# RWKV-7 stage of a one-core hybrid block: token shift, key scaling and decays read PSUM or go through ScalarE

## The chip, the core and the metric

One core of one Trainium2 chip runs one transformer block in fp32: sequence 1024, model width 1024. The metric is the device time of the whole program in microseconds, the median of the runs taken. TensorE multiplies, VectorE and ScalarE and GpSimd work on rows of 128 partitions, and DMA queues move data between HBM and the on-chip memory SBUF. TensorE writes its results to PSUM, a memory of eight banks of 128 x 512 fp32, from which VectorE and ScalarE read them.

In the profile the engines are PE (TensorE matmul), PEld (its weight loads), DVE (VectorE), ACT (ScalarE), POOL (GpSimd) and SP. L424 is line 424 of the kernel, `rkv<-rraw` an output and its inputs by the program's names.

## The reference

The block is an RMS norm, one wide input projection, three mixers side by side (NSA attention, RWKV-7, a gated delta network called GDN), gates that merge them, an output projection and a feed-forward part. The change touches the RWKV-7 mixer alone:

```python
c = c + (_shift(c) - c) * mu                       # token shift of r, k, v, wd, ad, gd
r, k, v, wd, ad, gd = jnp.split(c, splits, axis=-1)
w = -jax.nn.softplus(-(w0 + jnp.tanh(wd) @ w_up)) - 0.5
decay = jnp.exp(-jnp.exp(w))
a = jax.nn.sigmoid(a0 + ad @ a_up)
g = jax.nn.sigmoid(gd) @ g_up
kk = _l2n(heads(k * k_k))
k = k * (1.0 + (a - 1.0) * k_a)
# scan over the tokens, a 64 x 64 state per head, 8 heads:
sa = jnp.einsum('bhij,bhj->bhi', state, -kk_t)
state = state * w_t + sa (kk_t * a_t) + v_t k_t
y_t = jnp.einsum('bhij,bhj->bhi', state, r_t)
# then a norm of y per head, the bonus sum(r * k * r_k) * v, and times g
```

`_shift` moves a sequence by one token and puts zero first, so the shift is `c[t] + (c[t-1] - c[t]) * mu`, the same as `c[t] * (1 - mu) + c[t-1] * mu`.

## The kernel before

Every dense fp32 product is made of three fp32r matmuls, from operands split into a high and a low part. The weights come by DMA (`wraw`), ScalarE casts the high part (`whi`, L254) and GpSimd, here and there VectorE, subtracts for the low part (`wlo`, L259). A projection tile is 128 columns by half the sequence, 512 tokens: two loads of weights with 12 matmuls each (4 slices of the depth times 3) into one PSUM bank called `fps`. Two banks serve for `fps`, two for the general tiles `mps` with the tag "m", and one each for four others.

The RWKV stage lies at about 50 to 600 us of the span. `mixed` (L419) makes one of its 28 projection tiles, 14 column tiles by two halves: two for the low-rank inputs `wa` and `gd`, then r, k and v for two groups of head pairs (`pp` 0 and 1). When a half is complete, `take` copies it from PSUM to `rraw` (L424, ScalarE), puts the last column of the half before in front (L425), keeps its own last column (L427), and VectorE forms the difference of neighbours (L428) and multiplies and adds (L429) to give `rkv`, `wa` or `gd`. There is one `rraw` buffer.

`_rwkv_unit` treats 256 tokens of one group; there are eight units, `u = 4 * pp + q`. A unit

- makes the decays: two small products with sigmoids (L506) give `sg` and `av`, a scan within chunks of 64 (`tensor_tensor_scan`, L511) gives `cs`, GpSimd subtracts `sg` from `cs` for the sum up to the token before (L513), and ScalarE's exponentials give `sg`, `AG`, `WI` and `wc` (L520 to L524);
- once its r and k are there, makes `kk` (L531), its square `sq` (L533), the first rows of `AG` (L537, L538), the scaled key `k2`, which the profile calls `k` (L541, L542), `rk` and `kk * av` on GpSimd (L544, L545), and the chunk-relative keys `BK` from `k2` and `kk` times `WI` (L550);
- on TensorE sums `sq` and `rk` over the heads and multiplies `AG` by `BK` (results taken at L585 to L587), inverts a triangular matrix per chunk by blocks, and runs the recurrence over the chunks (`VS` at L682, L699, L705), then the norm of the output.

Nobody writes the order by hand. The units are generators (`Task`). A planner, `run` with `dense_step`, resumes the unit that is due, using a clock of estimated TensorE time and the waits in the table `LAT`, and puts steps of the dense projections between them, in the share that `BESIDE` gives. Then a scheduler, which simulates the engines' time, sets the order of each engine's instructions. All engines work through their instructions in that order and wait at each for its inputs and for its output's buffer. Besides RWKV's own projections, the dense work between the units is that of GDN and the other branches.

Buffers that the change touches: `SABUF = 5` for the rotating 128 x 512 tiles `sg`, `cs`, `WI`, `kk`, `sq`, `k2`, `rk`; the single `rraw`; and the "m" banks.

Of the kernel before, what the change touches and what calls it, by code (L numbers as in the profile page):

```python
# [19 lines left out]
P = 128  # L20
# [13 lines left out]
KAPPA = math.exp(-0.5)  # L34
# [77 lines left out]
class Block:  # L112
# [82 lines left out]
    def constants(self):  # L195
        nc, c, a = self.nc, self.const, self.a
# [23 lines left out]
        for n, k in (("nsa_q_norm", 1), ("nsa_k_norm", 3)):  # L220
# [159 lines left out]
    def rwkv(self):  # L380
        nc, tc, a, wk = self.nc, self.tc, self.a, self.wk
        col = self.col

        gmask = self.tl("gmask", 1, [P, 2, 64])
        m16 = self.tl("m16", 1, [P, 64])
        for i in range(2):
            t, base = gmask[:, i], -i
# [5 lines left out]
        for t, blk in ((m16, 16),):  # L393
            nc.gpsimd.memset(t, 0.0)
            for h in range(2):
# [3 lines left out]
                for b in range(1, 64 // blk, 2):  # L399
# [4 lines left out]
                                            base=b * blk - 1, channel_multiplier=-1)  # L404
        cmask = self.tl("cmask", 1, [P, P])
# [47 lines left out]
        consts = (gmask, m16, cmask, sums)  # L453
        shared = {}
# [16 lines left out]
    def _rwkv_unit(self, u, jobs, rkv, wa, gd, consts, shared):  # L471
# [36 lines left out]
        sg, av = sgav
        cs = ta("cs")
        for x in (slice(i * P, i * P + P) for i in range(4)):  # L510
            nc.vector.tensor_tensor_scan(out=cs[:, x], data0=cmask, data1=sg[:, x], initial=0.0, op0=OP.mult, op1=OP.add)  # L511
        csc = ch(cs)
# [12 lines left out]

# [1089 lines left out]
```

## Time and profile before

| | |
|---|---|
| runs (3) | 2533.8, 2536.28, 2540.54 us; median 2536.28 |
| profiled execution | 2527.64 us, of which the span is 2525.9 |
| PE | 2377.5 us busy, 94% of the span |
| PEld | 1907.6 us, 76% |
| DVE | 1472.0 us, 58% |
| ACT | 1043.1 us, 41% |
| POOL | 986.8 us, 39% |
| mean granted TensorE clock | 0.965 |

The chain that ended last, followed back from the last instruction, lies to 72% on PE and to 13% on DVE. The span holds one profiled execution. A view by windows gives each engine's busy time in a stretch and the share of full speed that TensorE's clock was granted there; a view of waits gives how long an engine stood still and for whose result; a view by groups gives the mean duration of one kind of instruction.

### The profile page before, as it was taken

The page shows a single profiled execution, that of the slowest core. Times are in us where ns is not written, and L with a number is a line of the kernel's source. Part 1 is how long each engine was busy: PE and PEld are TensorE (multiplying, and loading weights), DVE is VectorE, ACT ScalarE, POOL GpSimd, SP SyncE. Part 2 cuts the span into 40 slices and gives each one's busy share as a digit, 9 for nine tenths or more (in the row PEclk, how much of TensorE's full clock was granted, in tenths as well). Part 3 has the DMA queues.
Part 4 walks back from the last instruction along what each step waited for, and adds up shares of the span by engine and source line. Part 5 has one row for each costly group of instructions (what it writes and reads, how often), then busy time and mean ns, then how long its engine had stood idle before and what let it go on. Part 6 is the DMA issues. An engine that isn't in the chain of part 4 may idle for free.

```text
span 2525.9 us, 37184 instructions
## 1 busy us (share of the span) xinstructions
PE 2377.5 (94%) x13589; PEld 1907.6 (76%) x13589; DVE 1472.0 (58%) x3197; ACT 1043.1 (41%) x2083; POOL 986.8 (39%) x975
## 2 busy tenths in 40 slices
PE   6979899999988999989999999999999998999999
PEld 4757676777776777777887777778888876788887
DVE  4586877663477567232556777766454436545444
ACT  5333433332344433225657665654332334423232
POOL 4444444333322121224545675344333346233232
PEclk9889889999999999989999999999999999999999
DMA  4222222222223122272213331014232354223232
GB/s 137 68 56 65 58 63 58 71 54 74 72 66 83 43 57 73 83 173 80 64 52 114 111 106 57 21 62 128 92 109 84 117 164 157 75 88 111 83 111 92
DMA packets 319718, 216.79 MB, mean 86 GB/s; under 512 B 78486, under 2 KB 273184, under 8 KB 319536
## 3 DMA queue, kind: packets, MB, share of 16 engines
q1 hardware_dynamic: 308672, 195.63, 27.3%
q10 hardware_dynamic: 9792, 17.83, 2.0%
q8 instruction: 107, 1.75, 0.3%
q0 software_dynamic: 1072, 0.96, 0.2%
q14 instruction: 75, 0.61, 0.1%
HBM read 178.16 MB, written 36.22 MB: 85 GB/s over the span
## 4 chain that ended last, share of the span: by engine, by line
PE 72%; DVE 13%; DMA 6%; ACT 4%; issue 2%; POOL 2%; SPq 0%; ACTq 0%; POOLq 0%; DVEq 0%
PE fps L97 53%; PE mps L97 15%; PE mps L101 3%; DVE inv_p L336 2%; DVE inv_u L338 1%; DVE gacc L882 1%; DVE BK L550 1%; DMA cw<-in_nsa_cmp_w_dram 1%; POOL wlo L259 1%; DMA lb<-inv 1%; ACT P L1349 1%; ACT whi L254 1%; DMA wraw<-in_w_branch_dram 1%; DVE ast L1344 1%; DMA gin<-gates 1%
## 5 line engine op out<-in xcount | busy, mean ns | idle before, releaser
L259 POOL TENSOR_TENSOR wlo<-wraw,whi 128x512 fp32r<-128x512 f32 (+2 forms) x408 | 530.0, 1302 | 878.9 <-ACT whi L254 848.5
L254 ACT CAST whi<-wraw 128x512 fp32r<-128x512 f32 (+1 forms) x408 | 286.6, 705 | 632.1 <-PE fps L97 444.8
L97 PE MATMUL fps<-hTh,whi 128*128 128x512 f32 x1024 | 447.3, 439 | 6.5 <-ACT rraw L424 3.5
L97 PE MATMUL fps<-hTh,wlo 128*128 128x512 f32 x1024 | 415.8, 410 | 1.3 <-POOL wlo L259 1.3
L97 PE MATMUL fps<-hTl,whi 128*128 128x512 f32 x1024 | 416.5, 408 | 0.0
L259 DVE TENSOR_TENSOR wlo<-wraw,whi 128x256 fp32r<-128x256 f32 (+1 forms) x207 | 129.7, 629 | 232.5 <-ACT whi L254 227.0
L97 PEld LDWEIGHTS fps<-hTh,whi 128*128 128x128 f32 x1024 | 200.9, 197 | 48.5 <-ACT rraw L424 3.6
L97 PEld LDWEIGHTS fps<-hTh,wlo 128*128 128x128 f32 x1024 | 200.0, 196 | 47.7 <-POOL wlo L259 2.2
L97 PEld LDWEIGHTS fps<-hTl,whi 128*128 128x128 f32 x1024 | 201.8, 197 | 32.3
L97 PE MATMUL fps<-h2h,whi 128*128 128x512 f32 x512 | 200.0, 391 | 1.3 <-DVE h2l L291 1.3
L1363 POOL TENSOR_SCALAR P<-P,ast 128x64 f32<-128x64 f32 (+5 forms) x128 | 137.2, 1088 | 160.0 <-DVE ast L1356 97.1
L97 PE MATMUL fps<-h2l,whi 128*128 128x512 f32 x512 | 199.6, 390 | 0.0
L97 PE MATMUL fps<-h2h,wlo 128*128 128x512 f32 x512 | 199.4, 390 | 0.0
L97 PE MATMUL fps<-whi,fl 128*128 128x512 f32 x512 | 191.0, 389 | 0.0
L97 PE MATMUL fps<-whi,fh 128*128 128x512 f32 x512 | 189.9, 391 | 0.0
L97 PE MATMUL fps<-wlo,fh 128*128 128x512 f32 x512 | 189.0, 389 | 0.0
L1442 DVE TENSOR_TENSOR acc<-fps,acc 128x512 f32<-128x512 f32 x160 | 106.7, 686 | 101.4 <-PE fps L97 101.0
L1349 ACT ACTIVATE P<-mps,ast 128x128 f32<-128x128 f32 (+4 forms) x256 | 124.9, 494 | 75.3 <-DVE ast L1347 45.5
L1344 DVE TENSOR_REDUCE ast<-mps 128x1 f32<-128x128 f32 (+4 forms) x256 | 109.0, 441 | 56.3 <-PE mps L97 53.5
L1392 DVE TENSOR_TENSOR PL<-mps,PH 128x512 fp32r<-128x512 f32 (+2 forms) x168 | 103.3, 619 | 47.7 <-ACT PH L1391 47.0
L1391 ACT CAST PH<-mps 128x512 fp32r<-128x512 f32 (+2 forms) x168 | 88.1, 533 | 63.5 <-PE mps L101 58.1
L97 PEld LDWEIGHTS fps<-h2h,whi 128*128 128x128 f32 x512 | 96.2, 188 | 21.5 <-DVE h2l L291 1.8
(465 smaller groups left out, 4802.0 us busy)
## 6 DMA issues: line engine op xcount, KB each, us to landing
wraw<-in_w_in_dram SPq DMA_DIRECT2D x152, 256.0 KB, 2.9
wraw<-in_w_ff_dram SPq DMA_DIRECT2D x128, 256.0 KB, 2.8
wraw<-in_w_ff_dram SPq DMA_DIRECT2D x64, 512.0 KB, 3.4
gates<-fst ACTq DMA_DIRECT2D x48, 256.0 KB, 2.0
wraw<-in_w_branch_dram SPq DMA_DIRECT2D x48, 256.0 KB, 3.2
gin<-gates SPq DMA_DIRECT2D x48, 256.0 KB, 3.2
wraw<-in_w_out_dram SPq DMA_DIRECT2D x16, 512.0 KB, 3.5
nsa_in<-fst ACTq DMA_DIRECT2D x20, 256.0 KB, 2.1
```

The source lines that it names most:

```text
L97: return self.note(self.nc.tensor.matmul(out, lhsT=lhsT, rhs=rhs, **kw))
L101: return self.note(self.nc.tensor.transpose(out, x, ident))
L254: nc.scalar.copy(hi, raw)
L259: eng.tensor_tensor(out=lo[:, x], in0=raw[:, x], in1=hi[:, x].bitcast(F32), op=OP.subtract)
L336: nc.vector.tensor_tensor(out=v, in0=lt[:n, s, None, s + 1:].to_broadcast([n, w, w]), in1=u[:n, s + 1:, s + 1:].rearrange("p t c -> p c t" ...
L338: nc.vector.tensor_reduce(out=u[:n, s, s + 1:], in_=v, axis=AX, op=OP.add)
L1344: nc.vector.tensor_reduce(out=(mx if i == 0 else mx2)[:, b:b + 1], in_=ps[:, :n], axis=AX, op=OP.max, negate=True)
L1349: nc.scalar.activation(out=Pt[:, c:c + n], in_=tiles[i][:, :n], func=AF.Exp, bias=mx[:, b:b + 1], accum_out=(sm if i == 0 else sm2)[:, b:b ...
L1363: eng.tensor_scalar(out=Pt[:, c:c + n], in0=Pt[:, c:c + n], scalar1=r[:, b:b + 1], scalar2=None, op0=OP.mult)
L1391: nc.scalar.copy(PH[:n, x0:x1], ps[:n, x0:x1])
L1392: tt(out=PL[:n, x0:x1], in0=ps[:n, x0:x1], in1=PH[:n, x0:x1].bitcast(F32), op=OP.subtract)
L1442: tt(out=acc[:, st, c0:c0 + 512], in0=ps, in1=acc[:, st, c0:c0 + 512], op=OP.add)
```

## The change

Token shift: ScalarE now writes `ps * (1 - mu)` from PSUM straight to the output (L434 of the changed kernel), and one VectorE instruction adds `mu` times the same PSUM bank moved by one column (L439). The first column of the second half comes from the edge by one ScalarE instruction (L438). `rraw` and the subtraction are gone. The PSUM bank is thus read by VectorE as the last reader. `1 - mu` and `1 - k_a` are made once at the start.

Decays: the sigmoids and the scan write tiles with a zero column ahead of every chunk (`sgl`, `csl`, 65 columns per chunk, one buffer each), so the sum up to the token before is the same tile read one column to the left, and GpSimd's subtraction is dropped.

Key scaling: `kk` goes from VectorE to ScalarE (L542). `k2` is `av * k_a + (1 - k_a)` on ScalarE (L552), then one multiplication by `k` on VectorE (L555). `WI`'s exponential goes into a PSUM bank with the tag "m", later in the unit (L554), and the `BK` products read it there (L563). `SABUF` falls from 5 to 4.

```diff
-SABUF = 5
+SABUF = 4
...
+        less = c.tile([P, 18], F32, name="less")
+        self.col["less_mu"], self.col["less_k_a"] = less[:, 0:14], less[:, 14:18]
...
+            for n, o in (("rwkv_mu", "less_mu"), ("rwkv_k_a", "less_k_a")):
+                nc.vector.tensor_scalar(out=self.col[o], in0=self.col[n], scalar1=-1.0, scalar2=1.0, op0=OP.mult, op1=OP.add)
...
+        cmask = self.tl("cmask", 1, [P, 2, 65])
         nc.gpsimd.memset(cmask, 1.0)
-        nc.gpsimd.memset(cmask.rearrange("p (c t) -> p c t", t=64)[:, :, 0:1], 0.0)
+        nc.gpsimd.memset(cmask[:, :, 0:1], 0.0)
+        lead = [self.tl(n, 1, [P, 8, 65]) for n in ("sgl", "csl")]
+        nc.gpsimd.memset(lead[0][:, :, 0:1], 0.0)
...
             def take(ps, half):
-                raw, o = self.tl("rraw", 1, [P, 513]), out(half)
-                nc.scalar.copy(raw[:, 1:513], ps)
-                nc.scalar.copy(raw[:, 0:1], edge)
+                o = out(half)
+                nc.scalar.activation(out=o, in_=ps, func=AF.Copy, scale=less)
                 if half == 0:
-                    nc.scalar.copy(edge, raw[:, 512:513])
-                nc.vector.tensor_tensor(out=o, in0=raw[:, 0:512], in1=raw[:, 1:513], op=OP.subtract)
-                nc.vector.scalar_tensor_tensor(out=o, in0=o, scalar=col["rwkv_mu"][:, ct:ct + 1], in1=raw[:, 1:513],
+                    nc.scalar.copy(edge, ps[:, 511:512])
+                else:
+                    nc.scalar.activation(out=o[:, 0:1], in_=edge, func=AF.Identity, scale=mu, bias=o[:, 0:1])
+                nc.vector.scalar_tensor_tensor(out=o[:, 1:512], in0=ps[:, 0:511], scalar=mu, in1=o[:, 1:512],
                                                op0=OP.mult, op1=OP.add)
...
-            o = ta("sg")
+            o = ch(ta("av")) if y else sgl[:, :, 1:65]
...
+        for i in range(4):
+            x = slice(2 * i, 2 * i + 2)
+            nc.vector.tensor_tensor_scan(out=flat(csl[:, x]), data0=flat(cmask), data1=flat(sgl[:, x]), initial=0.0,
+                                         op0=OP.mult, op1=OP.add)
...
-        nc.gpsimd.tensor_sub(sg, cs, sg)
...
-        WI = ta("WI")
+        sg = ta("sg")
...
-        nc.scalar.activation(out=sg, in_=sg, func=AF.Exp, scale=-KAPPA)
+        nc.scalar.activation(out=ch(sg), in_=before, func=AF.Exp, scale=-KAPPA)
...
-        nc.scalar.activation(out=WI, in_=cs, func=AF.Exp, scale=KAPPA)
...
-            ts(out=pr(kk)[:, x], in0=k[:, x], scalar1=one("rwkv_k_k", x), scalar2=None, op0=OP.mult)
+            nc.scalar.activation(out=pr(kk)[:, x], in_=k[:, x], func=AF.Copy, scale=one("rwkv_k_k", x))
...
-            ts(out=pr(k2)[:, x], in0=pr(av)[:, x], scalar1=1.0, scalar2=one("rwkv_k_a", x), op0=OP.subtract, op1=OP.mult)
-        stt(out=pr(k2), in0=pr(k2), scalar=1.0, in1=k, op0=OP.add, op1=OP.mult)
+            nc.scalar.activation(out=pr(k2)[:, x], in_=pr(av)[:, x], func=AF.Identity, scale=one("rwkv_k_a", x), bias=one("less_k_a", x))
+        WI = ps_tile()
+        nc.scalar.activation(out=ch(WI), in_=cs, func=AF.Exp, scale=KAPPA)
+        tt(out=pr(k2), in0=pr(k2), in1=k, op=OP.mult)
```

How the instructions of VectorE stand in a row at the first unit's keys, before (`k_854` is this unit's k2, `rkv` the r, k and v tiles):

```order
L428 TENSOR_TENSOR rkv<-rraw 128x512
L429 SCALAR_TENSOR_TENSOR rkv<-rkv,pcol,rraw 128x512
L531 TENSOR_SCALAR kk<-rkv,pcol 128x256
L428 TENSOR_TENSOR rkv<-rraw 128x512
L429 SCALAR_TENSOR_TENSOR rkv<-rkv,pcol,rraw 128x512
L531 TENSOR_SCALAR kk<-rkv,pcol 128x256
L537 SCALAR_TENSOR_TENSOR AG<-sg,kk 64x4x64 x4
L541 TENSOR_SCALAR k_854<-sg,pcol 128x256 x2
L542 SCALAR_TENSOR_TENSOR k_854<-k_854,rkv 128x512
L550 TENSOR_TENSOR BK<-kk,WI 64x8x64 x2
L550 TENSOR_TENSOR BK<-k_854,WI 64x8x64 x2
```

and in the changed kernel, from the tile that completes k to the last `BK` (`k_833` is k2, the `mps` read by L563 is `WI`):

```order
L439 SCALAR_TENSOR_TENSOR rkv<-fps,pcol,rkv 128x511 x2
L549 TENSOR_TENSOR AG<-rkv,AG 128x4x64 x2
L439 SCALAR_TENSOR_TENSOR rkv<-fps,pcol,rkv 128x511 x2
L548 SCALAR_TENSOR_TENSOR AG<-sg,kk 64x4x64 x4
L555 TENSOR_TENSOR k_833<-k_833,rkv 128x512
L563 TENSOR_TENSOR BK<-k_833,mps 64x8x64 x2
L563 TENSOR_TENSOR BK<-kk,mps 64x8x64 x2
L439 SCALAR_TENSOR_TENSOR rkv<-fps,pcol,rkv 128x511 x2
```

L428, L531 and L541 are gone from the row, L555 and L563 stand where L542 and L550 stood, and `AG` comes before one of the shift's instructions instead of behind it.

ScalarE at the same place before, from the last of unit 0's tiles that it copies to the square `sq`:

```order
L424 COPY rraw<-fps 128x512
L427 COPY edge<-rraw 128x1
L254 CAST whi<-wraw 128x512
L425 COPY rraw<-edge 128x1
L533 ACTIVATE sq<-kk 128x512
L254 CAST whi<-wraw 128x512
L424 COPY rraw<-fps 128x512
```

and in the changed kernel:

```order
L434 ACTIVATE rkv<-fps,less 128x512
L436 COPY edge<-fps 128x1
L542 ACTIVATE kk<-rkv,pcol 128x256
L259 CAST whi<-wraw 128x512 x2
L434 ACTIVATE rkv<-fps,less 128x512
L436 COPY edge<-fps 128x1
L542 ACTIVATE kk<-rkv,pcol 128x256
L259 CAST whi<-wraw 128x512
L544 ACTIVATE sq<-kk 128x512
L552 ACTIVATE k_833<-av,less,pcol 128x256 x2
```

`kk` and `k2` have joined ScalarE's row, with the casts of the next projections' weights among them; a shift tile is one L434 and one L436 where it was L424, L427 and L425.

VectorE at the start of the stage, before (`g_*` are GDN's decays, `wa` the first shift tile):

```order
L825 SCALAR_TENSOR_TENSOR g_p<-g_p,g_z 128x32
L827 SCALAR_TENSOR_TENSOR g_x<-g_p,g_x 128x32
L829 SCALAR_TENSOR_TENSOR g_g<-g_x,hc 128x32
L428 TENSOR_TENSOR wa<-rraw 128x512
L429 SCALAR_TENSOR_TENSOR wa<-wa,pcol,rraw 128x512
L682 COPY VS<-Z_640 64x2x64 x2
L428 TENSOR_TENSOR wa<-rraw 128x512
L429 SCALAR_TENSOR_TENSOR wa<-wa,pcol,rraw 128x512
```

and in the changed kernel:

```order
L838 SCALAR_TENSOR_TENSOR g_p<-g_p,g_z 128x32
L840 SCALAR_TENSOR_TENSOR g_x<-g_p,g_x 128x32
L842 SCALAR_TENSOR_TENSOR g_g<-g_x,hc 128x32
L439 SCALAR_TENSOR_TENSOR wa<-fps,pcol,wa 128x511 x2
L695 COPY VS<-Z_635 64x2x64 x2
L521 SCALAR_TENSOR_TENSOR csl<-cmask,sgl 128x130 x2
```

The shift of `wa` keeps its place behind the `g_*` row; it is now the instruction that frees the `fps` bank.

## Rows read from the trace of the kernel before

**Rows 1.** Window: length, busy PE, PEld, DVE, ACT, POOL, clock, DMA share, GB/s

```profile
50.00:600.00 550.00, 509.10 (x3907) 383.58 (x3909) 395.61 (x947) 196.24 (x378) 228.29 (x241) 0.92 0.26 63
```

**Rows 2.** PE's waits, 50 to 600 us: total us, times, longest us

```profile
PE mps L97 <- DVE VS L699: 8.0, 6, 2.4
PE mps L97 <- DVE BK L550: 7.4, 3, 4.0
PE mps L97 <- POOL rk L544: 5.2, 2, 3.5
...
PE fps L97 <- ACT rraw L424: 3.5, 1, 3.5
PE mps L97 <- DVE VS L682: 2.3, 1, 2.3
```

**Rows 3.** Windows at the start, behind stalls, without one (columns as rows 1)

```profile
53.00:60.00 7.00, 6.88 (x23) 5.52 (x24) 5.55 (x21) 1.53 (x6) 3.96 (x14) 0.76 0.15 34
60.00:70.00 10.00, 10.00 (x47) 7.30 (x46) 3.89 (x7) 8.07 (x17) 2.85 (x3) 1.00 0.11 27
108.00:122.00 14.00, 14.00 (x43) 10.32 (x43) 7.03 (x19) 1.53 (x5) 3.60 (x3) 0.51 0.15 37
145.00:153.00 8.00, 6.56 (x26) 5.50 (x26) 7.75 (x20) 0.19 (x1) 2.53 (x2) 0.57 0.25 66
278.00:293.00 15.00, 12.15 (x78) 10.24 (x79) 11.48 (x24) 3.58 (x7) 6.50 (x8) 0.54 0.25 56
408.00:419.00 11.00, 10.68 (x75) 9.17 (x76) 7.12 (x20) 3.27 (x5) 1.39 (x1) 0.53 0.14 35
508.00:562.00 54.00, 51.41 (x468) 38.11 (x467) 37.13 (x100) 19.74 (x34) 20.15 (x23) 1.00 0.27 63
```

**Rows 4.** DVE groups, 50 to 600 us: busy us, mean ns, idle before, releaser

```profile
L428 DVE TENSOR_TENSOR rkv<-rraw 128x512 f32<-128x512 f32 x24 | 25.2, 1051 | 20.5 <-ACT rraw L424 20.2
...
L429 DVE SCALAR_TENSOR_TENSOR rkv<-rkv,pcol,rraw 128x512 f32<-128x512 f32 x24 | 22.5, 939 | 0.6
L550 DVE TENSOR_TENSOR BK<-k,WI 64x512 f32<-64x512 f32 x16 | 20.0, 1248 | 0.4
L550 DVE TENSOR_TENSOR BK<-kk,WI 64x512 f32<-64x512 f32 x16 | 18.4, 1152 | 0.3
...
L541 DVE TENSOR_SCALAR k<-sg,pcol 128x256 f32<-128x256 f32 x16 | 14.8, 967 | 0.0
...
L531 DVE TENSOR_SCALAR kk<-rkv,pcol 128x256 f32<-128x256 f32 x16 | 8.1, 532 | 0.1
...
L542 DVE SCALAR_TENSOR_TENSOR k<-k,rkv 128x512 f32<-128x512 f32 x8 | 6.5, 809 | 0.2
```

**Rows 5.** Single lines: min/median/max ns, first and last start us, shape

```profile
L726 DVE TENSOR_TENSOR Y<-Y,gst x8: 676/693/1815, 226.0 to 631.9; 128x512 f32<-128x512 f32 x8
...
L631 DVE TENSOR_TENSOR T<-mps,T x8: 673/690/693, 172.7 to 591.4; 128x512 f32<-128x512 f32 x8
...
L291 DVE SCALAR_TENSOR_TENSOR hTl<-mps,gain,hTh x16: 735/750/753, 14.9 to 39.6; 128x512 fp32r<-128x512 f32 x16
...
L290 ACT ACTIVATE hTh<-mps,gain x16: 666/687/690, 13.6 to 38.9; 128x512 fp32r<-128x512 f32 x16
```

**Rows 6.** ACT groups, 50 to 600 us (columns as in rows 4)

```profile
L254 ACT CAST whi<-wraw 128x512 fp32r<-128x512 f32 x70 | 43.2, 617 | 111.0 <-PE fps L97 97.1 <-issue 6.4 <-DMA wraw<-in_w_in_dram 5.5
L424 ACT COPY rraw<-fps 128x512 f32<-128x512 f32 x28 | 16.2, 580 | 0.1
L506 ACT ACTIVATE sg<-mps,pcol 128x256 f32<-128x256 f32 x32 | 14.5, 473 | 11.2 <-PE mps L97 10.9
...
L425 ACT COPY rraw<-edge 128x1 f32<-128x1 f32 x28 | 5.3, 189 | 55.4 <-DVE rkv L429 44.3 <-DVE n L566 6.8 <-DVE n L567 2.7
```

**Rows 7.** DVE timeline at the start: start us, us, engine, line

```profile
56.18 0.22 DVE L829 SCALAR_TENSOR_TENSOR g_g<-g_x,hc 128x32 f32<-128x32 f32 x1
```

**Rows 8.** PE timeline at the start: idle before and releaser in brackets

```profile
53.12 0.50 PE L97 MATMUL fps<-hTh,whi 128*128 128x512 f32 x1 [3.50 <-ACT rraw L424]
```

More of the change, by code (lines that the diff above doesn't have):

```diff
@@ L404, in rwkv @@
                                             base=b * blk - 1, channel_multiplier=-1)
-        cmask = self.tl("cmask", 1, [P, P])
+        cmask = self.tl("cmask", 1, [P, 2, 65])
         nc.gpsimd.memset(cmask, 1.0)
-        nc.gpsimd.memset(cmask.rearrange("p (c t) -> p c t", t=64)[:, :, 0:1], 0.0)
+        nc.gpsimd.memset(cmask[:, :, 0:1], 0.0)
+        lead = [self.tl(n, 1, [P, 8, 65]) for n in ("sgl", "csl")]
+        nc.gpsimd.memset(lead[0][:, :, 0:1], 0.0)
         sums = self.tl("sums", 1, [P, 5, 2])
@@ L416, in rwkv @@
         edges = self.tl("edge", 1, [P, 14])
-        nc.gpsimd.memset(edges, 0.0)
         def mixed(ct, out, halves=(0, 1)):
             edge = edges[:, ct:ct + 1]
+            mu, less = col["rwkv_mu"][:, ct:ct + 1], col["less_mu"][:, ct:ct + 1]
             def take(ps, half):
-                raw, o = self.tl("rraw", 1, [P, 513]), out(half)
-                nc.scalar.copy(raw[:, 1:513], ps)
-                nc.scalar.copy(raw[:, 0:1], edge)
+                o = out(half)
+                nc.scalar.activation(out=o, in_=ps, func=AF.Copy, scale=less)
                 if half == 0:
-                    nc.scalar.copy(edge, raw[:, 512:513])
-                nc.vector.tensor_tensor(out=o, in0=raw[:, 0:512], in1=raw[:, 1:513], op=OP.subtract)
-                nc.vector.scalar_tensor_tensor(out=o, in0=o, scalar=col["rwkv_mu"][:, ct:ct + 1], in1=raw[:, 1:513],
+                    nc.scalar.copy(edge, ps[:, 511:512])
+                else:
+                    nc.scalar.activation(out=o[:, 0:1], in_=edge, func=AF.Identity, scale=mu, bias=o[:, 0:1])
+                nc.vector.scalar_tensor_tensor(out=o[:, 1:512], in0=ps[:, 0:511], scalar=mu, in1=o[:, 1:512],
                                                op0=OP.mult, op1=OP.add)
@@ L452, in rwkv @@
                         jobs[pp, half].append(self.job(mixed(2 * pp + x + i * 4, out, (half,)), ready))
-        consts = (gmask, m16, cmask, sums)
+        consts = (gmask, m16, cmask, sums, lead)
         shared = {}
@@ L475, in _rwkv_unit @@
         mark = self.mark
-        gmask, m16, cmask, sums = consts
+        gmask, m16, cmask, sums, (sgl, csl) = consts
         wk, ps_tile = self.wk, self.mps
@@ L501, in _rwkv_unit @@
             ps = ps_tile()
-            o = ta("sg")
+            o = ch(ta("av")) if y else sgl[:, :, 1:65]
             for x in range(2):
-                xs = slice(x * 256, x * 256 + 256)
-                self.te.matmul(ps[:, xs], lhsT=up[HH[y], x], rhs=wa[HH[y]], start=True, stop=True)
-                nc.scalar.activation(out=o[:, xs], in_=ps[:, xs], func=AF.Sigmoid, bias=one(n, x))
+                self.te.matmul(ps[:, x * 256:x * 256 + 256], lhsT=up[HH[y], x], rhs=wa[HH[y]], start=True, stop=True)
+                nc.scalar.activation(out=o[:, 4 * x:4 * x + 4], in_=ch(ps)[:, 4 * x:4 * x + 4], func=AF.Sigmoid, bias=one(n, x))
             sgav.append(o)
[L508 to L512, printed above, removed]
-        nc.gpsimd.tensor_sub(sg, cs, sg)
+        av = sgav[1].rearrange("p c t -> p (c t)")
+        flat = lambda ap: ap.rearrange("p c t -> p (c t)")
+        for i in range(4):
+            x = slice(2 * i, 2 * i + 2)
+            nc.vector.tensor_tensor_scan(out=flat(csl[:, x]), data0=flat(cmask), data1=flat(sgl[:, x]), initial=0.0,
+                                         op0=OP.mult, op1=OP.add)
+        cs, before = csl[:, :, 1:65], csl[:, :, 0:64]
+        cs2 = cs.rearrange("p (x c) t -> p x c t", x=2)
         AG = [self.tl("AG", AGBUF, [P, 2, 2, 3, 64]) for _ in range(2)]
-        WI = ta("WI")
+        sg = ta("sg")
         wc = wk.tile([P, 8], F32, name="wc", tag="wc", bufs=3)
         q2 = (slice(0, 2), slice(2, 4))
-        nc.scalar.activation(out=sg, in_=sg, func=AF.Exp, scale=-KAPPA)
+        nc.scalar.activation(out=ch(sg), in_=before, func=AF.Exp, scale=-KAPPA)
         for ag, c2 in zip(AG, q2):
-            nc.scalar.activation(out=ag[:, :, :, 2], in_=ch2(cs)[:, :, c2], func=AF.Exp, scale=-KAPPA)
-        nc.scalar.activation(out=WI, in_=cs, func=AF.Exp, scale=KAPPA)
-        nc.scalar.activation(out=wc, in_=csc[:, :, 63], func=AF.Exp, scale=-KAPPA)
+            nc.scalar.activation(out=ag[:, :, :, 2], in_=cs2[:, :, c2], func=AF.Exp, scale=-KAPPA)
+        nc.scalar.activation(out=wc, in_=cs[:, :, 63], func=AF.Exp, scale=-KAPPA)
         yield lambda: all(j.done for j in jobs[:4])
```

## The prediction

> **What bounds the kernel now.** I read the stage windows first. From 50 to 600 us, where the RWKV units run, TensorE is busy 509.1 of 550 us, so it sets the pace, but it loses time in two ways: 40.9 us idle, and a mean granted clock of 0.92, which is 0.08 x 550 = 44 us of full-speed work [rows 1]. No other engine is near its limit there: VectorE 395.6, ScalarE 196.2, GpSimd 228.3 us. A cheaper instruction elsewhere is therefore worth only what it takes out of a TensorE wait. TensorE's list of waits says which these are: VS L699 8.0 us in six pieces, BK L550 7.4 in three, rk L544 5.2 in two, rraw L424 3.5 in one, VS L682 2.3 in one [rows 2]. L550 and L544 end the chain that the change shortens (from the projected k to kk, k2, rk and BK); L424 is the token shift, which it rewrites; L699 is the state recurrence, which it leaves alone.
>
> The windows behind the chain's stalls show what a stall costs beyond itself. [...] Lost there: 14 x 0.49 + 8 x 0.43 + 15 x 0.46 + 11 x 0.47 = 22.4 us. The waits (7.4 + 5.2 + 2.3 = 14.9 us) and these stretches make **37.3 us** that the touched chain can give back at most.
>
> **The change part by part.** *VectorE, token shift.* The subtraction L428 goes: 24 x 1051 ns for rkv, and four for wa and gd at about that price, 29 us. L429 (939 ns) now reads one operand from PSUM [rows 4]. Instructions with both operands in SBUF stretch here, from 676 up to 1815 ns at L726, an ordinary 128x512 one. PSUM readers do not: L631, 128x512 with one operand in PSUM, stays within 673 to 693 over eight runs, and L291, which has the new L439's form (PSUM, pointer, SBUF), within 735 to 753 [rows 5]. So I price L439 at 0.75 and each BK product at 0.69 instead of 1.25 and 1.15.
>
> [...]
>
> *VectorE, kk and k2.* L531 (16 x 532) and L541 (16 x 967) leave for ScalarE. What changes between k and BK in one unit was 2 x 0.53 + 2 x 0.97 + 0.81 + 2 x 1.25 + 2 x 1.15 = 8.6 us on VectorE (L531, L541, L542, L550) [rows 4]; it becomes 0.75 (L555, where L631's 0.69 is the lower bound) + 4 x 0.69 = 3.5. That is **5.1 us less per unit**, against a longest wait of 4.0 [rows 2]. Over the stage VectorE loses 29 + 28 x 0.19 + 8 x 5.1 = 75 of its 396 us. Nearly all of that is worth nothing by itself, since VectorE is not the bound.
>
> *ScalarE.* A 128x512 tile from PSUM takes 580 ns as a copy (L424) and 687 with a scale from a pointer (L290): 107 for the pointer [rows 5, 6]. L506, 128x256 with one pointer, takes 473. So kk costs 0.47 and k2, with two pointers, 0.58: 16 x 1.05 = 16.8 us; the shift 28 x 0.107 = 3.0 more; 14 edge copies of 0.19 fewer, -2.7. ScalarE goes from 196 to about 213 of 550 us, no bound. But kk and k2 now stand in a queue of casts that wait for TensorE: 111.0 us idle before 70 casts, 1.6 each [rows 6]. By the order one to three casts lie among kk and k2, and rk, BK and so TensorE wait behind them. Bounds: 0 to 3 x 1.6 = 4.8 us per unit. I take one, 1.6, since a cast that waits for an earlier TensorE step is often past when k arrives. With k2's own 1.2 beside VectorE's 3.6 us of AG work (L548, L549, unchanged) the chain gains 3.5 us, as much as the longer of the two waits for rk and all but 0.5 of the longest for BK.
>
> *GpSimd.* L513, one subtraction per unit, goes. The exp that read it reads the scan shifted by a column instead. That runs long before kk in the order, and TensorE's waits name neither. The scans grow from 128 to 130 columns. Priced at zero; if their cover went, they would lie ahead of AG, which rk and BK do not read.
>
> *PSUM.* WI takes one of two "m" banks from its exp to the last BK product. Worst, TensorE waits for a bank through four products, 8 units x 2.8 = 22 us; best, zero, since the next tiles wanted are the sums and AG x BK, which wait for the same rk and BK anyway. I take +1.
>
> *The fps banks.* Here the change adds a wait. Before, L424 on ScalarE frees a projection's bank. After, L439 on VectorE does, and whatever is ahead of it on VectorE delays TensorE. Before, ScalarE's L425 waited 44.3 us, over 28 tiles 1.6 each, for L429 [rows 6]: VectorE does lag, and TensorE does not see it. A bank is wanted again some 24 matmuls later, at 10.0 / 47 = 0.21 us each 5.1 us [rows 3]; minus 0.69 + 0.75 for the two instructions, 3.7 us of lag are free. One place has no such room: the first bank, wa's. VectorE is in another branch's decay chain (g_*) until 56.18 + 0.22 = 56.40 [rows 7]. gd's first matmul, now at 53.12 after 3.50 us of waiting [rows 8], then waits for 56.40 + 0.75 = 57.15: **+4.1 us** if the orders hold; the clock behind it is low already (0.76 over 7 us [rows 3]). Bounds: 0.9 (L439 ready as early as it could be, 53.12 + 0.11 + 0.75) to 6.
>
> *The sum.* 37.3, minus half of the third stretch (a wait for rk of 5.2 - 3.5 = 1.7, the 2.3 for L682 and 6.9 of clock, 10.9 together), as L682 belongs to the state and may stay: 31.9 us won. Lost: 4.1 at the start, 1 for the bank. **-26.8 us**: the profiled execution of 2527.6 us (span 2525.9 and 1.7 around it) goes to 2501, and the median of the runs, 2536.3, which stands 8.6 above it, to **2509.5**.
>
> **The rivals.** *ScalarE eats the gain.* If three casts, not one, hold up kk and k2, 4.8 of the 5.1 us are gone; the waits move to ScalarE's names, and most of the low stretches stay. At 40% of 31.9, less 5.1: -7.7, 2528.6. For it: those 111 us. Against: the casts wait while TensorE works, and only what is late at the chain's end counts. [...]
>
> *The time moves into the state's chain.* The unit's products come earlier, but L699 (8.0 us, longest 2.4) takes over the stalls with the low clock behind them, because the inverse in between takes as long as before. Then a quarter of the 31.9 lasts, less 5.1: about -3, 2533.
>
> *Slower: the banks.* L439's lag passes 3.7 us, not at the start alone but wherever VectorE holds an inverse or a unit's chain. Each such tile costs some 2 us and 1.7 of clock behind it (7 us at 0.76 behind the 3.5 us stall [rows 3]). It decides from 26.8 / 3.7 = 8 of the 28 tiles on; at ten it is +10, 2546. For it: where the lag shows, it is of the order of the room. Against: much of it was L428 and the single rraw buffer, both gone.
>
> *More than summed.* VectorE with 75 us less also shortens the L699 waits and what lies behind them: 8.0 us more, -35, 2501, and 2492 with as much again in clock.
>
> That the change does not do what it says is excluded by the order: L428, L513 and VectorE's rows of kk and k2 are gone.
>
> **How the numbers follow.** My forecast 0.5, ScalarE 0.17, the state's chain 0.12, the banks 0.11, more than summed 0.10. A measurement of this kernel tells some 0.3%, 7.6 us, from no change: below 2528.7 is faster, above 2543.9 slower. The forecast and "more than summed" are faster (0.60), and so are two thirds of ScalarE's case (0.11), which lies on that edge; the rest of it, the state's chain and the smaller half of the banks' cases are the same (0.21), and slower is 0.08. The range reaches from "more than summed" with its clock, 2492, to the state's chain with 2 us on it, 2535; it leaves out the banks and a little below.
>
> **What the changed profile would show.** TensorE's waits without BK and rk, or under 3 us together; a wait of 7 to 8 us for wa L439 before gd's first matmul; a granted clock above 0.95 from 50 to 600 us; L563 near 0.69; VectorE near 320 us in the stage. ScalarE's names (kk L542, k2 L552) or other L439 tiles in TensorE's waits, or a clock still at 0.92, would make it wrong.

## The result, and the profile after

The changed kernel takes **2496.4 us** (median of four runs, 2491.6 to 2502.8) where the kernel before took 2536.1 (four runs); these medians divide to 0.9844. The ratio on record is 0.9863, with a 95% interval of 0.984 to 0.9887, and timed again, five runs against 17 of the kernel before, it was 0.9862 (0.9835 to 0.9888). I go by these: 1.4% faster, some 35 us. The forecast was 2509.5, a gain of 26.8 us, with a range of 2492 to 2535: right in sign and inside the range, short in size by 13 us of the medians, 8 by the ratio. The profiled execution took 2491.6 us (span 2489.5), 36.1 less than the one of before. All ratios leave out three disturbed executions (2622, 4975 and 6582 us), one each of "keys alone", "WI alone" and "keys and WI".

The stretch from 50 to 600 us of the changed kernel, with the columns of [rows 1]:

```profile
50.00:600.00 550.00, 522.59 (x4154) 391.94 (x4154) 328.52 (x916) 218.28 (x406) 216.36 (x244) 0.95 0.27 67
```

TensorE idles 27.4 us there instead of 40.9, at a granted clock of 0.95 instead of 0.92 (0.94 in a second execution). VectorE went from 395.6 to 328.5 us (forecast: near 320), ScalarE from 196.2 to 218.3 (forecast: 213).

All of TensorE's waits in that stretch (who waited for what: us in total, times, longest), to be held against [rows 2]:

```profile
PE mps L97 <- DVE VS L712: 7.8, 10, 2.1
PE fps L97 <- DVE wa L439: 7.5, 1, 7.5
PE mps L97 <- DVE U L669: 2.4, 1, 2.4
PE mps L97 <- DVE VS L718: 2.0, 3, 1.2
PE mps L97 <- DMA T<-inv: 1.8, 2, 1.6
PE fps L97 <- POOL wlo L264: 1.2, 2, 0.6
PE mps L97 <- ACT sq L544: 0.9, 1, 0.9
PE mps L97 <- DVE xs L703: 0.9, 2, 0.5
PE fps L97 <- ACT whi L259: 0.8, 1, 0.8
PE mps L97 <- ACT U L653: 0.6, 1, 0.6
PE mps L97 <- DVE X L662: 0.6, 1, 0.6
PE fps L97 <- ACT fst L327: 0.4, 1, 0.4
PE mps L101 <- ACT ab L783: 0.3, 1, 0.3
```

What the list does not have is the point: BK (7.4 us), rk (5.2) and the state's VS L682 (2.3) are gone. What it has anew is one wait of 7.5 us for wa's L439, which takes the place of the 3.5 us for L424 of [rows 8]. It ends here (timeline of TensorE):

```profile
57.76 0.79 PE L97 MATMUL fps<-hTh,whi 128*128 128x512 f32 x1 [7.46 <-DVE wa L439]
```

The groups of VectorE from 50 to 600 us that answer to L429, the two L550 and L542 of [rows 4] (busy us, mean ns, idle before and its releaser):

```profile
L439 DVE SCALAR_TENSOR_TENSOR rkv<-fps,pcol,rkv 128x511 f32<-128x511 f32 x24 | 17.9, 747 | 28.3 <-ACT edge L436 20.7 <-ACT rkv L434 7.3
...
L563 DVE TENSOR_TENSOR BK<-kk,mps 64x512 f32<-64x512 f32 x16 | 11.0, 685 | 1.3 <-POOL kk L558 1.0
L563 DVE TENSOR_TENSOR BK<-k,mps 64x512 f32<-64x512 f32 x16 | 10.9, 684 | 0.3
...
L555 DVE TENSOR_TENSOR k<-k,rkv 128x512 f32<-128x512 f32 x8 | 7.0, 872 | 3.3 <-ACT k L552 3.2
```

Both instructions that read PSUM cost what the bounds said, 0.75 and 0.69 us. L555, whose two operands are still in SBUF, costs 0.87, not 0.75.

**Where the time went.** To compare the runs I take the stretch from 45 us to the first product of the GDN stage (gZ x KQ) and split it: TensorE's idle time, the clock loss (1 minus the granted clock, times the length, over pieces of 25 us), and the rest, which is work at full clock. Idle time at low clock counts in both of the first two, 2 to 5 us of it in the kernels before and after. One execution of each kernel:

```profile
45.00:670.77 625.77, 579.07 (x4317) 436.45 (x4316) 419.26 (x1000) 215.61 (x410) 257.63 (x302) 0.92 0.26 64
```

is the kernel before, and this the changed one:

```profile
45.00:639.07 594.07, 560.83 (x4321) 421.68 (x4319) 342.88 (x940) 232.02 (x429) 235.12 (x294) 0.95 0.27 68
```

Idle fell from 46.7 to 33.3 us, clock loss from 47.5 to 27.9, and the rest stayed (531.6 and 532.9). So 31.7 us were won by the end of the stage, two fifths as idle and three fifths as clock. The end of the span moved by 36.4. The other 4.7 us came behind the stage, where the change touches nothing; in a second execution of the changed kernel only 1.1 us did, so that is spread between executions. The second execution gave 34.0 us idle and 32.5 of clock loss, so the clock's part is known to some 5 us.

### The profile page after: what moved, and what is told of

Its sections match the earlier page's. It is cut to its first block, busy times and chain, and to the rows that moved or that the text cites. A ratio compares the mean times of both kernels' runs of the same rounds, so it can differ in the third digit from the quotient of the medians.

```text
span 2489.5 us, 37131 instructions
## 1 busy us (share of the span) xinstructions
PE 2357.2 (95%) x13589; PEld 1891.7 (76%) x13589; DVE 1396.8 (56%) x3139; ACT 1060.3 (43%) x2101; POOL 965.8 (39%) x967
## 4 chain that ended last, share of the span: by engine, by line
PE 77%; DVE 10%; DMA 5%; ACT 4%; issue 2%; POOL 1%; SPq 1%; ACTq 0%; DVEq 0%; POOLq 0%
PE fps L97 57%; PE mps L97 16%; PE mps L101 4%; DVE inv_p L341 2%; DVE inv_u L343 1%; DMA cw<-in_nsa_cmp_w_dram 1%; DVE gacc L895 1%; DMA lb<-inv 1%; DMA wraw<-in_w_branch_dram 1%; ACT P L1362 1%; DMA inv<-LT 1%; DVE ast L1357 1%; POOL wlo L264 0%; ACT whi L259 0%; DVE ast L1360 0%
## 5 line engine op out<-in xcount | busy, mean ns | idle before, releaser
L97 PE MATMUL fps<-hTh,whi 128*128 128x512 f32 x1024 | 442.5, 434 | 10.5 <-DVE wa L439 7.5
L97 PEld LDWEIGHTS fps<-hTl,whi 128*128 128x128 f32 x1024 | 199.7, 195 | 32.5 <-issue 0.3
```

Source lines behind the costliest of these rows:

```text
L97: return self.note(self.nc.tensor.matmul(out, lhsT=lhsT, rhs=rhs, **kw))
```

## Experiments

**Theory and rivals.** The theory of the prediction, *chain*: the gain comes from a shorter way from k to rk and BK, by way of TensorE's waits for them and the low clock behind. Its rivals: *load*, the time follows VectorE's busy time in the stage, whatever is cut; and *operand*, only the BK products' move to PSUM, away from GpSimd, counts. After the first four runs a fourth was formed, *plan*: TensorE's order is planned with undisturbed durations, and it is enough to plan for the real ones. Ratios are to runs of the kernel before on the same chip (medians 2530.5 to 2532.8 us there).

| kernel | ratio (95% interval) | idle, us | clock loss, us | VectorE busy, us |
|---|---|---|---|---|
| before | 1 | 46.7 | 47.5 | 419 |
| shift alone | 1.0038 (1.0022 to 1.0054) | 54.8 | 44.7 | 386 |
| keys alone | 1.0009 (0.9987 to 1.0031) | 47.8 | 60.0 | 400 |
| WI alone | 0.9925 (0.9908 to 0.9943) | 46.9 | 27.2 | 402 |
| keys and WI | 0.9919 (0.9899 to 0.9939) | 39.6 | 32.5 | 387 |
| before, products later | 1.0039 (1.0024 to 1.0054) | 53.3 | 49.2 | 422 |
| changed, keys undone | 0.9963 (0.9936 to 0.999) | 46.1 | 39.2 | 366 |
| changed, WI undone | 0.9974 (0.9952 to 0.9996) | 48.5 | 44.5 | 370 |
| changed, k2 late | 0.992 (0.9895 to 0.9945) | 39.3 | 60.0 | 349 |
| changed | 0.9863 (0.984 to 0.9887) | 33.3 | 27.9 | 343 |

The last three columns are of the stretch to gZ x KQ in one execution each. The rest of it is 530 to 538 us in all rows but two: "products later" (549), where 50 more projection matmuls stand ahead of its end, and "k2 late" (522), whose profiled execution was also the longest of its runs (2496 to 2521 us). Why the account is some 10 us out there is open.

**The shift alone.**

```diff
-                nc.scalar.copy(raw[:, 1:513], ps)
...
-                nc.vector.tensor_tensor(out=o, in0=raw[:, 0:512], in1=raw[:, 1:513], op=OP.subtract)
...
+                nc.scalar.activation(out=o, in_=ps, func=AF.Copy, scale=less)
```

> The kernel before with the new token shift alone (no subtraction L428, VectorE reads the bank; kk, k2, decays and WI as before). Chain theory: what counts is the time from k to rk and BK; it gets shorter by the interleaved L428s only, some 2.5 us, so of the four stalls (1.9, 3.5 + 1.4, 1.8 and 4.0 us) about 9 us of waiting goes, with 10 to 15 us of low clock behind; the start costs 4.1 more: 2512 to 2521 us, with waits of 1 to 2 us for rk or BK left in the second and sixth unit. Load theory: the gain of 39.6 us goes with VectorE's 67 us less work in the stage; the shift is 34 of them: half of it, 2516. Operand theory (WI in PSUM carries the gain): little, 2530 or more. The wait for wa's bank of 7 to 8 us is there in all three.

Measured: 2541.2 us, slower than before by 0.4%, and outside what either theory gave. The waits of TensorE from 50 to 600 us, first rows:

```profile
PE mps L97 <- DVE VS L704: 10.7, 7, 2.3
PE fps L97 <- DVE wa L434: 7.5, 1, 7.5
PE mps L101 <- POOL Y L740: 5.5, 5, 2.2
PE mps L97 <- DVE VS L710: 5.4, 4, 1.8
PE mps L97 <- DVE BK L555: 4.8, 3, 3.9
```

VectorE lost 33 us of work and nothing was won: *load* falls. BK still stalls TensorE, at the first unit for 3.9 us instead of 1.9. In TensorE's order its first AG x BK stands there behind 230 projection matmuls; before, and in the changed kernel, behind 240. With a shorter chain the scheduler put the product earlier, while the key products still took 1.0 to 1.3 us each beside GpSimd.

**Keys and WI, without the shift.** kk and k2 on ScalarE, WI in PSUM, the old shift and decays.

```diff
-        nc.scalar.activation(out=WI, in_=cs, func=AF.Exp, scale=KAPPA)
...
+            nc.scalar.activation(out=pr(kk)[:, x], in_=k[:, x], func=AF.Copy, scale=one("rwkv_k_k", x))
...
+        WI = ps_tile()
+        nc.scalar.activation(out=WI, in_=cs, func=AF.Exp, scale=KAPPA)
```

> The kernel before with the key part alone: kk and k2 on ScalarE, one multiplication left for k2, WI's exponential in a PSUM bank and BK read from there; the old token shift with its copy and the old decays with GpSimd's subtraction. Chain theory: the chain loses 5.1 us per unit and the waits for rk and BK go but for some 0.5 us each, with their low clock, 25 to 32 us; no loss at the start (the wait for L424 stays 3.5 us): 2502 to 2511. Load theory: 40 of 67 us of VectorE work gone, 24 us: 2512. Operand theory: all of the gain, without the start's loss: 2492.

Measured: 2512.0 us, ratio 0.9919: 20 us faster than before; *chain* expected 25 to 32 and *load* 24, so this run alone does not tell them apart. The trace is of a second execution:

> One look at the kernel before with the key part alone (timed already at 0.992), whose first trace was of a disturbed execution. If the shift's part of the gain (0.992 to 0.986) lies in TensorE's waits and clock, idle and clock loss of the stage stand between those of before (47 and 48 us) and of the changed kernel (33 and 28), and the waits for rk and BK are small.

Idle 39.6 and clock loss 32.5 us: both between before and changed. rk is left with 1.3 us, BK with 0.2. The wait at the start is the old 3.5. So the other 14 us (0.9919 to 0.9863) come with the shift and the decays, of which the shift alone costs time; the decays were not run alone.

**k2 late.** The changed kernel with k2 formed three times over on ScalarE.

```diff
-        for x in range(2):
+        for x in (0, 1) * 3:
             nc.scalar.activation(out=pr(k2)[:, x], in_=pr(av)[:, x], func=AF.Identity, ...
```

> The changed kernel with k2 computed three times over on ScalarE, that is 4 x 0.55 = 2.2 us more in each unit's chain ahead of rk and BK, and no work more on VectorE. Chain theory: the trace of the changed kernel leaves 1.3 us of room in the first unit, 0.1 to 0.7 in the second, 1.3 in the fourth and the sixth, over 2.7 in the others, so stalls of 0.9, 2, 0.9 and 0.9 us come back, and behind each 3 to 7 us of low clock: 8 to 25 us slower than the changed kernel, 2505 to 2521, with rk or BK in TensorE's waits. Load theory and operand theory: within 3 us of the changed kernel's 2496, since only ScalarE, at 218 of 550 us, works more.

Measured: 2515.2 us, ratio 0.992: 14 us behind the changed kernel by the ratios, and inside *chain*'s 2505 to 2521. VectorE has the same 940 instructions: *load* falls again. But the stalls came elsewhere than expected: rk took only 1.6 us of waiting, as the scheduler moved the second unit's AG x BK from 314 to 336 projection matmuls; the loss is in the clock (60 us) and in waits behind it (the inverse's DMA 5.3, casts 3.3).

**WI back in SBUF**, written in place over the scan's tile.

```diff
-        WI = ps_tile()
-        nc.scalar.activation(out=ch(WI), in_=cs, func=AF.Exp, scale=KAPPA)
+        nc.scalar.activation(out=cs, in_=cs, func=AF.Exp, scale=KAPPA)
+        WI2 = cs2
...
```

> The changed kernel with WI's exponential written in place over the scan's tile in SBUF, so that BK's products have both operands in SBUF again and the second 'm' bank is free. Chain theory: each product goes from 0.69 to about 1.2 us where GpSimd works beside it, 2 us per unit at most against rooms of 0.1 to 3 us: one to three small stalls, 3 to 13 us slower than the changed kernel, 2499 to 2509. Load theory: 16 us of VectorE work come back, 9 us: 2505. Operand theory: 20 us or more slower, above 2516. Were the bank missed in the changed kernel, this one would be faster than 2496.

Measured: 2523.4 us, ratio 0.9974. Undoing this one part takes four fifths of the gain away, as *operand* said and *chain* did not. VectorE's groups of BK, 50 to 600 us:

```profile
L563 DVE TENSOR_TENSOR BK<-k,csl 64x512 f32<-64x512 f32 x16 | 20.7, 1292 | 0.4
...
L563 DVE TENSOR_TENSOR BK<-kk,csl 64x512 f32<-64x512 f32 x16 | 18.1, 1131 | 2.0 <-ACT k L552 1.2 <-POOL kk L558 0.6
```

The products go from 0.68 back to 1.13 and 1.29 us, and TensorE waits for BK 4.4 us, for the inverse's DMA 5.7, for sq 4.1. The free "m" bank brings nothing visible. The traces show the lengths product by product, against GpSimd's work beside them. In the kernel before, 9 of the 32 BK products have no GpSimd instruction beside them and take 0.67 to 0.69 us; the other 23 take 1.40 on average and up to 2.14. With WI back in SBUF it is 8 at 0.67 to 0.69 and 24 at 1.39. In the changed kernel 30 of 32 have a GpSimd instruction beside them and still take 0.67 to 0.69. So the length of the products does not come from writing in place; whether that costs time elsewhere was not told apart.

**WI alone**, on the kernel before.

```diff
-        WI = ta("WI")
...
+        WI = ps_tile()
+        nc.scalar.activation(out=WI, in_=cs, func=AF.Exp, scale=KAPPA)
```

> The kernel before with WI's exponential in a PSUM bank and BK read from there, nothing else. Plan theory: BK's products take 0.69 as planned instead of 1.25 and 1.15, 2 us per unit, and the scheduler puts the second unit's products 12 matmuls later; the waits for BK (7.4 us) shrink to some 3, those for rk (5.2 us) only in the second unit: 8 to 18 us faster than before, ratio 0.993 to 0.997. Load theory: 16 us of VectorE work less, 9 us: 0.9965. Operand theory: most of the gain, below 0.990.

Measured: 2514.6 us, ratio 0.9925, 19 us, just beyond the expected 8 to 18 and short of *operand*'s 0.990. TensorE's waits from 50 to 600 us, first rows:

```profile
PE mps L97 <- DVE VS L699: 10.5, 10, 2.2
PE mps L97 <- DVE VS L705: 5.2, 4, 2.0
PE mps L97 <- DMA T<-inv: 4.8, 3, 2.3
PE fps L97 <- ACT rraw L424: 3.5, 1, 3.5
PE mps L97 <- DVE U L656: 2.7, 1, 2.7
```

Of BK 0.3 us is left in the whole list, of rk nothing, yet idle time in the stage is 46.9 us where it was 46.7: the state (VS 8.0 to 10.5, 3.8 to 5.2), the inverse's DMA (0.8 to 4.8) and U (0.6 to 2.7) took it over. What is won is the clock, 47.5 to 27.2 us. This is the second rival of the prediction, half of it: much of the idle time does move into the state's chain, the low clock does not move with it. WI's tile also leaves the five buffers that it shared with others; no run held that apart, but in the run before this one those buffers are used as in the changed kernel, and the gain went with the products' length.

**Keys alone**, kk and k2 on ScalarE, WI in SBUF.

```diff
-            ts(out=pr(kk)[:, x], in0=k[:, x], scalar1=one("rwkv_k_k", x), scalar2=None, op0=OP.mult)
+            nc.scalar.activation(out=pr(kk)[:, x], in_=k[:, x], func=AF.Copy, scale=one("rwkv_k_k", x))
...
```

> The kernel before with kk and k2 on ScalarE alone; BK still reads WI from SBUF, the old shift. TensorE's order has the second unit's products 10 matmuls later than before. The waits for rk should go (k2's pair is off VectorE's chain), those for BK stay in part, as its products still take 1.2 us; as in the kernels with later products, part of the gain returns as waits for the state (VS): 5 to 18 us faster than before, ratio 0.993 to 0.998. If the key part needs WI in PSUM to gain at all, 1.00.

Measured: 2531.0 us, ratio 1.0009: nothing. The waits for rk fall from 5.2 to 1.0 us as expected; those for BK stay (the first two rows of TensorE's list, 50 to 600 us):

```profile
PE mps L97 <- DVE VS L704: 11.7, 9, 2.6
PE mps L97 <- DVE BK L555: 6.3, 3, 3.2
```

**Keys undone**, kk and k2 back on VectorE in the changed kernel.

```diff
+            ts(out=pr(kk)[:, x], in0=k[:, x], scalar1=one("rwkv_k_k", x), scalar2=None, op0=OP.mult)
...
+            ts(out=pr(k2)[:, x], in0=pr(av)[:, x], scalar1=one("rwkv_k_a", x), scalar2=one("less_k_a", x), op0=OP.mult, op1=OP.add)
```

> The changed kernel with kk and k2 back on VectorE (k2 as av x k_a + (1 - k_a) in one instruction), all else as changed. Plan theory: their real durations (0.53 and 0.97 us a piece, undisturbed 0.33) exceed the plan by 1.7 us per unit, as the products' places in TensorE's order are those of the changed kernel to within 5 matmuls; rooms of 0.1 to 1.3 us in four units are overrun: 8 to 18 us slower than the changed kernel, ratio to the kernel before 0.990 to 0.994. Load theory: 23 us of VectorE work come back, 13 us of time: 0.992. If ScalarE's queue cost what it saves, no difference: 0.986.

Measured: 2521.7 us, ratio 0.9963: 25 us of the gain go, more than any theory gave. Waits for BK come back with 2.5 us, for the inverse's DMA with 6.6 and for sq with 4.9. A part that wins nothing alone is worth 25 us as the last one: the parts have to come together.

**Products later in the plan**, on the kernel before: one number.

```diff
-LAT = (0.0, 10.0, 0.2, 0.3, 0.1, 16.0, 1.2, 1.2, 1.2, 1.2, 1.0, 9.0, 4.0)
+LAT = (0.0, 12.0, 0.2, 0.3, 0.1, 16.0, 1.2, 1.2, 1.2, 1.2, 1.0, 9.0, 4.0)
```

> The kernel before, with one number changed: the planner's wait between a unit's BK and its products on TensorE, 10.0 to 12.0 us. No instruction is added or removed; in TensorE's order the first AG x BK of units 2 to 8 stands behind 12 to 48 more projection matmuls (3 to 10 us) than before. Plan theory (formed from the first four runs): the stalls before rk and BK come because TensorE's order is planned with undisturbed durations, and VectorE's chain takes longer than planned where both operands lie in SBUF beside GpSimd; the change gains because its chain keeps to the plan, and moving the products behind the real chain does the same: the waits for rk and BK go in all units but the first (AG x BK stays behind 240 matmuls there, 1.9 us), 15 to 30 us faster than before, ratio 0.988 to 0.994. Chain theory: shorter work is needed for the gain; products that start later end later, every unit by 3 to 10 us, and the stage is no shorter: ratio 1.00 or above. Load theory: 1.00.

Measured: 2543.1 us, ratio 1.0039 (1.0024 to 1.0054). BK is left with 1.9 us at the first unit and rk with none, as *plan* said, and the time still rose. TensorE's first rows, 50 to 600 us:

```profile
PE mps L97 <- DVE VS L699: 18.6, 11, 2.8
PE fps L97 <- POOL wlo L259: 4.7, 3, 4.0
PE mps L97 <- ACT U L640: 3.7, 2, 3.3
```

The waits for the state's L699 more than doubled (8.0 to 18.6 us). *Plan* falls in this form: products that start later end later, and the recurrence behind them then holds TensorE. One setting was run, and the durations that the scheduler itself goes by were left as they were.

**The start.** GDN's decays behind the first two shift tiles, in the changed kernel:

```diff
             self.scratch()
-            self.gdn_small()
...
         self.finish(self.job(mixed(12, lambda half: wa[half])), self.job(mixed(13, lambda half: gd[half])))
+        self.gdn_small()
```

> The changed kernel with the GDN decays (g_*) computed behind the first two shift tiles instead of ahead of the stage; the same work in another place. The wait for wa's bank before gd's first matmul, 7.5 us in the changed kernel, should fall to 2 to 3 us, since ScalarE's and VectorE's instructions for wa then stand ahead of the g_* chain: 4 to 7 us faster than the changed kernel, ratio to the kernel before about 0.984. If that wait was hidden anyway, no difference, 0.986.

Measured: 2492.1 us, ratio 0.9837 (0.9802 to 0.9871). The wait fell to 3.3 us:

```profile
51.22 0.71 PE L97 MATMUL fps<-hTh,whi 128*128 128x512 f32 x1 [3.29 <-DVE wa L439]
```

Then the sigmoid of the attention gates moved as well:

```diff
-        nc.scalar.activation(out=self.gs, in_=gates, func=AF.Sigmoid)
...
         self.gdn_small()
+        nc.scalar.activation(out=self.gs, in_=self.gs, func=AF.Sigmoid)
```

> The changed kernel with the GDN decays and the sigmoid of the attention gates (gs) behind the first shift tiles, so that wa's two ScalarE instructions stand ahead of every table load. The wait for wa's bank should be 1.5 to 2.5 us where it was 7.5 in the changed kernel and 3.3 with the decays alone moved: 5 to 8 us faster than the changed kernel's runs of the same call, ratio to the kernel before 0.982 to 0.985. If it only moves the stall (gd's own tile or the first unit waits instead), no difference.

and the changed kernel again beside it:

> The changed kernel as it is, beside the next one on the same chip: ratio to the kernel before 0.984 to 0.989 as in its first timing.

Measured: 2492.9 us, ratio 0.9845 (0.9814 to 0.9876), against 2497.0 and 0.9862 for the changed kernel. The wait is 1.9 us, and the first unit's AG x BK starts at 102.64 us instead of 109.03; the stage ends at 637.3 us, against 639.1 and 640.8. Both kernels beat the one before clearly, and the changed one by 4 us in the medians, within their intervals: that they are faster than it is likely and not shown. Idle time in the stretch to gZ x KQ is 29.6 and 27.1 us, against 33.3 and 34.0 in the two executions of the changed kernel, but their clock loss is 32.2 and 34.0, against 27.9 and 32.5: the shorter wait did not bring clock with it.

## Why the prediction was right, point by point

**The bound.** Right. With the work at full clock constant (531.6 and 532.9 us), the stage's time is TensorE's idle time plus its clock loss. VectorE's work as such was worth nothing: with the shift alone 33 us of it went, and the kernel was 0.4% slower (9 us, of which 4 are the longer wait at the start).

**The chain's waits and the clock.** The 12.6 us for BK and rk went to zero. From the start of its second kk to the end of its last BK, the first unit takes 8.1 us instead of 11.1, the second 10.5 instead of 16.7 and the sixth 17.0 instead of 20.9; these three had the longest waits, and the sum had 3.5 us for each. The clock was to give back the 22.4 us lost in the four low stretches of [rows 3], less 3.4 in the third, 19.0; it gave 19.6 by the accounts of one execution each. That this fits so well is in part luck. Behind the products of the first, second and sixth unit, where three of the four low stretches of [rows 3] lay, the clock is now full. Behind the fourth unit's, the stretch at 278 us there, it is not, for longer than before and without a stall (columns of [rows 3]):

```profile
108.00:122.00 14.00, 14.00 (x84) 11.29 (x83) 6.64 (x20) 3.59 (x8) 4.18 (x5) 1.00 0.29 73
139.00:147.00 8.00, 8.00 (x44) 6.54 (x43) 7.55 (x22) 2.22 (x4) 3.16 (x4) 1.00 0.26 68
387.00:398.00 11.00, 11.00 (x95) 8.35 (x95) 8.37 (x25) 3.07 (x6) 6.96 (x8) 1.00 0.18 51
270.00:287.00 17.00, 17.00 (x94) 12.04 (x93) 11.16 (x28) 3.75 (x9) 5.90 (x5) 0.51 0.11 32
```

So the four stretches gave back 22.4 - 8.4 = 14.0 us, and the other 5.6 came from low stretches that the prediction did not price; in the second execution the fourth unit's stretch is shorter, some 10 us at half clock. Of the signs that it named, TensorE's list without BK and rk, the wait for wa and L563 came as written; VectorE stands at 328.5 us and not near 320; and the clock, to be above 0.95, is so narrowly in one execution and not in the second (0.94).

**The start.** 57.15 us was forecast for gd's first matmul; it came at 57.76, after 7.46 us of waiting (7 to 8 forecast). The start-fix runs show that the reason was the one given: with the g_* row out of the way the wait is 3.3, then 1.9 us.

**Sizes on VectorE and ScalarE.** L439 0.747 (0.75), L563 0.685 (0.69), L555 0.872 (0.75): the one with two SBUF operands was sized too low. On ScalarE L434 took 0.684 (0.687), kk 0.496 (0.47), k2 0.593 (0.58).

**What was mis-sized.** The terms that I took off or added by half. L682's wait, kept at half of 2.3, vanished; the "m" bank, put at +1 us, shows in no wait; and small waits not counted fell too, L705's from 3.8 to 2.0, sg's 1.3 and G's 1.7 to nothing, which new ones for U, the inverse's DMA, sq and xs partly fill. Net idle fell 13.4 us where the sum had 14.9 - 2.0 (half of the third stretch's waits) - 5.1 = 7.8. These 5.6 us are about what the stage gave beyond the sum, 31.7 - 26.8 = 4.9. The state's VS waits together, 14.1 us before (L699, L705, L682), are 9.8 after and 11.5 in the second execution. That is the "more than summed" case in kind, at part of its size. The rest of the 13 us by the medians is spread: the forecast carried 8.6 us from the profiled execution to the median, and the changed kernel's were 4.9 apart. One sum is slightly off: the range's lower end, 2536.3 - 34.8 - 8.0, is 2493.5 and not 2492; the result lies above both.

**The queue on ScalarE.** The 1.6 us for a cast ahead of kk and k2 was the wrong reason where it counts. Between the second kk and k2 of the first two units ScalarE waits 0.14 us and nothing at casts; in the first it waits for VectorE instead (5.5 us of that over the eight units). In the other six it does stand before such casts, 2.9 to 11.4 us per unit, and still TensorE's list has no wait for rk or BK: those units had more room than the queue took. The first unit's and the fourth unit's rows of its timeline:

```profile
102.51 1.10 ACT L552 ACTIVATE k<-av,less,pcol 128x256 f32<-128x256 f32 x2 [1.58 <-DVE AG L548]
...
255.67 0.62 ACT L259 CAST whi<-wraw 128x512 fp32r<-128x512 f32 x1 [4.52 <-PE fps L97]
```

k2 needs nothing from L548 but the buffer that L548 reads last: with SABUF = 4, k2 gets sg's. I had not seen this, and that its size in the first unit is that of my term is chance. Moving kk and k2 back to VectorE costs 25 us in the changed kernel (0.9963 against 0.9863). Taken alone, in the kernel before, the move to ScalarE brings nothing (1.0009).

**The rivals.** ScalarE: neither kk nor k2 is in TensorE's list, only sq with 0.9 us. The banks: L439 delayed a bank at the start alone; no other shift tile is in TensorE's list. The state's chain: part of WI alone's idle time moved there, and it is what undoes the later plan. Why it did not hold back the whole change was argued and not shown: each part alone leaves either BK late (shift, keys) or the state's answers from VectorE late (WI), and together both may get shorter. Of the parts, WI in PSUM counts most, 0.75% alone and four fifths of the gain when undone. Why exactly the shift with the decays is worth 14 us behind the other parts, when the shift costs 10 alone, is not settled: its work on VectorE lies ahead of both chains, but each kernel also has its own order, and no run held the order fixed.

## What to carry to other kernels

Split a stage into work at full clock, idle and clock loss before pricing a change; here the first stayed within 7 us of the kernel before in all rows but two, and the clock carried more than the waits (19.6 us against 13.4, and 15.0 against 12.7 in the second execution). Where VectorE's products sit between TensorE's steps beside a busy GpSimd, look for an operand that can live in PSUM: here it made them as short as the planner believes (0.68 us instead of 1.13 to 1.29). Test parts together as well as alone: three parts at +0.4%, 0.1% and -0.7% made -1.4%, and look for who now frees a buffer or bank late.

## What the runs showed of the hardware that was not expected

Low clock came without a stall as well. In "k2 late" TensorE has no idle time from 200 to 270 us, and yet, with the columns of [rows 3]:

```profile
216.00:220.00 4.00, 4.00 (x34) 3.21 (x33) 3.19 (x6) 2.70 (x7) 2.52 (x2) 1.00 0.36 85
220.00:224.00 4.00, 4.00 (x49) 3.14 (x47) 3.88 (x10) 1.47 (x3) 2.17 (x3) 1.00 0.23 58
224.00:228.00 4.00, 4.00 (x22) 3.13 (x23) 3.52 (x12) 3.67 (x7) 1.77 (x2) 0.79 0.41 113
228.00:232.00 4.00, 4.00 (x16) 2.67 (x14) 2.19 (x5) 0.00 (x0) 0.72 (x1) 0.50 0.03 9
232.00:236.00 4.00, 4.00 (x48) 2.86 (x47) 0.71 (x2) 0.98 (x2) 2.27 (x3) 0.50 0.00 0
```

The granted clock goes from 1.00 to 0.50, and the matmuls of 512 columns go from 0.39 to 0.63 us in the timeline at 226.47. What TensorE did just before, from 223.20 to 225.4 us, are narrow products only:

```profile
223.20 0.69 PE L97 MATMUL mps<-T,LT 32*32 32x32 f32 x32
223.83 0.38 PE L97 MATMUL mps<-sums,rk 128*128 128x2 f32 x2
224.07 0.36 PE L97 MATMUL mps<-sums,sq 128*128 128x2 f32 x2
```

and five more like the last two; then come four wide matmuls, and with the next one the clock is low. It stays low for some 20 us, in which the wide matmuls start 0.43 us apart instead of 0.23: about 10 us lost by the account, though that account is 10 us out for this execution. In the changed kernel the same sums of that unit passed at full clock (1.00 from 194 to 242 us), but those of the fourth unit did not. TensorE has no idle time there from 257 to 287 us, the clock is 0.51 from 270 to 287 (the last row of the clock windows above), and just before it stand AG x BK, the sums and 32 products of this kind:

```profile
268.59 1.15 PE L97 MATMUL mps<-L,U 64*64 64x64 f32 x32
```

So in these two places a stretch of low clock began behind narrow products that follow one another, with no wait at all, and it did not in every order nor, by the spread of "k2 late" over 25 us, in every run. The prediction tied the low stretches to the stalls ahead of them; these two had none. That this separates orders that look nearly the same in the experiments above is likely, but was argued from these two places.
